# Neighbourhood bias masked on VectorE, the second layer's bias made in the first feed-forward, softmax maxima taken with the sign turned

## The chip, the cores and the metric

The kernel runs on one core of a Trainium2 chip. Its engines run side by side, each with its own queue in program order: PE (TensorE, matrix multiplications), DVE (VectorE), ACT (ScalarE), POOL (GpSimd) and SP (SyncE, here only the queue that issues transfers). The metric is the device time of one execution in microseconds; the median of the shown runs counts.

## The reference

Two identical layers act on 256 rows of width 1024. A layer is a mixer and a feed-forward with a gate, in float32:

```
h = rms_norm(x, n1);  proj = h @ w_in        # 1024 -> 2560, cut into qa ka va, qd kd vd, qc kc vc
out_a = neighbourhood_attention(rms(qa), rms(ka), va)        # 4 heads, a learned bias rpb per offset
out_d = dilated_window_attention(rot(rms(qd)), rot(rms(kd)), vd)   # 6 heads
out_c = gqa_block_attention(rot(rms(qc)), rot(rms(kc)), vc)        # 6 heads, 2 key heads
x = x + concat(rms(out_a), rms(out_d), rms(out_c)) @ w_out
h = rms_norm(x, n2);  g, u = split(h @ w_gate_up)            # 2 x 2816
x = x + (gelu(conv3(g)) * u) @ w_down
```

In all three attentions a score is q.k * 64^-0.5 plus a bias, and a softmax follows. The neighbourhood bias of a query and a key is rpb[head, row offset, column offset] inside a window of 16 columns, and minus infinity outside.

## The kernel before

**Arithmetic.** Every float32 weight or activation that goes to PE is split into a rounded part ("hi", cast by ACT) and the rest ("lo", subtracted by DVE), and a product takes two or three matmuls. Weights come in units of up to 1 MB through SP's queue into four `raw` buffers; a unit's split (`wp_hi`, `wp_lo`) is made while the unit two before it is multiplied.

**Stages of a layer.** First the norm's transposes (`act_hT`) and the projections dq, dk, dv, cq, ckv, aqk, av into PSUM banks `psa_a`. `normed` (line 840) makes each head's sum of squares (`small_ss`), on POOL the factor (`small_ms`, then `small_rstd` by a power), and on DVE the scaled `act_z`; `rotated` multiplies by cosine and sine tables that POOL makes from `const_rot` and the gains (`tables_d`, line 809: cdq, sdq, cdk, sdk; `tables_c`, line 824: ccq, scq, cck, sck). Then sixteen heads in the order 6 dilated ("d"), 6 grouped ("c"), 4 neighbourhood ("a"): scores in pairs into `psw_w`, softmax (`Head.softens`, line 942), transposes of the probabilities and their split (`act_ch`, `act_cl`), and the weighted sum with the values. Projections and output projections (`act_mixT`) fill PE between these. The feed-forward then runs eleven steps of gate, up and down.

**Softmax.** With a bias, one DVE operation (CUSTOM_DVE_ANT_0 in the profile, ISA in the lists of order below) adds it, scales, writes `act_s2k` and keeps the row's maximum, which a second small instruction writes to `small_mx`. Without one (group c) DVE reduces the maximum of the scores. For each head a DVE multiplication then makes `small_nm`, minus the maximum (times the scale in group c), which ACT's exponential takes as its bias. DVE's reciprocal and two ACT scalings finish the head.

**Neighbourhood bias of a layer.** `na_load` (line 692) brings 28 rows of 31 numbers (`act_few`); `na_repeat` (line 706) scales them on POOL by 8, copies them 64 times along the free axis into `act_nab` (28x1984) and writes that to a scratch in DRAM (`dram_scr`); `na_diagonals` (line 716) reads it back along diagonals with two transfers, so that each query partition has its bias for 28 (head, row offset) pairs and 64 columns. `na_bias_mask` (line 1076) adds the column mask `const_na` in three operations of 9x64 columns on POOL. There is one `act_nab` buffer; the second layer's is made from steps 2, 3 and 4 of the first feed-forward on in program order.

**What sets the order.** The kernel first records every operation with what it reads and writes (`Plan.add`, line 241). `Plan.order` (line 289) then lays the work out by list scheduling: of all operations that are ready it takes the one that can start first by its own cost function (`cost`, line 396) and handover times, ties by program position. `emit` (line 388) issues them in that order; line 393 is the line of nearly every instruction in the profile. So any changed cost or dependence can move work on every engine.

Of the kernel before, what the change touches and what calls it, by code (L numbers as in the profile page):

```python
# [11 lines left out]
F32 = mybir.dt.float32  # L12
F32R = mybir.dt.float32r
I32 = mybir.dt.int32
AF = mybir.ActivationFunctionType
# [200 lines left out]

class Plan:
    def __init__(self, tc):
        self.tc, self.ops, self.shift, self.burst, self.bursts = tc, [], 0, None, {}
        for name, short in (("tensor", "PE"), ("scalar", "ACT"), ("vector", "DVE"), ("gpsimd", "POOL"), ("sync", "SP")):  # L220
            setattr(self, name, PlanEngine(self, short, getattr(tc.nc, name)))

# [10 lines left out]
    @contextmanager  # L233
    def together(self):

        self.burst = len(self.bursts)
        self.bursts[self.burst] = []
        yield
        self.burst = None

    def add(self, engine, method, args, kw):
        o = Op()
# [37 lines left out]
            v.tile.reads.append((i, v.footprint()))  # L280
        for v in outs:
            v.tile.writes.append((i, v.footprint()))
        o.before.discard(i)
        o.left = len(o.before)
        for j in o.before:
# [150 lines left out]
def encoder_kernel(  # L436
# [268 lines left out]

    def na_repeat(l):
        rows_ = nabs[l].rearrange("p r c -> p (r c)")[:NR]
        nc.gpsimd.tensor_scalar(nabs["few"], nabs["few"], ISCALE, None, ALU.mult)
        nc.gpsimd.tensor_copy(
            rows_.rearrange("p (n c) -> p n c", c=RPB_C),  # L710
            nabs["few"].unsqueeze(1).to_broadcast([NR, GRID_W, RPB_C]),
        )
        nabs["scr"] = dram.tile([NR, GRID_W * RPB_C], F32, tag="scr", name=f"scr{l}")
        nc.sync.dma_start(nabs["scr"], rows_)

    def na_diagonals(l):
        scr = nabs["scr"]
        for i in range(2):
            nc.sync.dma_start(
                nabs[l][i * GRID_W : (i + 1) * GRID_W, i : i + NR],  # L720
                scr.strided(15, [[RPB_C - 1, GRID_W], [GRID_W * RPB_C, NR], [1, GRID_W]]),
            )

    load(0)
    for l in range(DEPTH):
# [68 lines left out]
        if l == 0:  # L794
# [9 lines left out]
            na_load(0)  # L804
            gq = gq.rearrange("p (l a d) -> p l a d", l=DEPTH, d=HD)
            gk = gk.rearrange("p (l a d) -> p l a d", l=DEPTH, d=HD)


        def tables_d(which, g):
            cd = act.tile([P, NT, HD], F32, tag=f"cd{which}", name=f"cd{which}{l}", bufs=1)  # L810
            sd = act.tile([P, NT, 16], F32, tag=f"sd{which}", name=f"sd{which}{l}", bufs=1)
            b = lambda v: v.unsqueeze(1).to_broadcast([P, NT, v.shape[1]])
            nc.gpsimd.tensor_tensor(cd, rot[:, :, 0:64], b(g[:, l, 1]), op=ALU.mult)
            for i in range(2):
                o, n = (8 * i, 8 * (1 - i)), 8
                nc.gpsimd.tensor_tensor(
                    sd[:, :, o[0] : o[0] + n],
                    rot[:, :, 64 + o[0] : 64 + o[0] + n],
                    b(g[:, l, 1, o[1] : o[1] + n]),
                    op=ALU.mult,  # L820
                )
            return cd, sd

        def tables_c(which, g):
            cc = act.tile([P, NT, HD], F32, tag=f"cc{which}", name=f"cc{which}{l}", bufs=1)
            sc = act.tile([P, NT, HD], F32, tag=f"sc{which}", name=f"sc{which}{l}", bufs=1)
            b = lambda v: v.unsqueeze(1).to_broadcast([P, NT, v.shape[1]])
            nc.gpsimd.tensor_tensor(cc, rot[:, :, 80:144], b(g[:, l, 2]), op=ALU.mult)
            for i in range(4):
                o, n = (16 * i, 16 * (i ^ 1)), 16  # L830
                nc.gpsimd.tensor_tensor(
                    sc[:, :, o[0] : o[0] + n],
                    rot[:, :, 144 + o[0] : 144 + o[0] + n],
                    b(g[:, l, 2, o[1] : o[1] + n]),
                    op=ALU.mult,
                )
            return cc, sc


        def normed(ps, nh, t, name):  # L840
# [96 lines left out]
        class Head:  # L937
# [4 lines left out]
            def softens(self, sps):  # L942

                name, bias = self.name, self.bias
                self.p = p = act.tile([P, NT, S], F32, tag="s2k", name=f"p_{name}", bufs=NS2K)
                nm = small.tile([P, NT], F32, tag="nm", name=f"nm_{name}")
                mx = small.tile([P, NT], F32, tag="mx", name=f"mx_{name}")
                rs = small.tile([P, NT], F32, tag="rs", name=f"rs_{name}")
                if bias is not None:
                    sb = act.tile([P, NT, S], F32, tag="s2k", name=f"sb_{name}", bufs=NS2K)  # L950
                    for t in range(NT):
                        nc.vector.tensor_tensor_reduce(
                            sb[:, t], sps[t], bias[t], SCALE, -3e38, ALU.add, ALU.max, mx[:, t : t + 1]
                        )
                    nc.vector.tensor_scalar_mul(nm, mx, -1.0)
                    for t in range(NT):
                        nc.scalar.activation(
                            p[:, t], sb[:, t], AF.Exp, bias=nm[:, t : t + 1], accum_out=rs[:, t : t + 1]
                        )
                else:  # L960
                    for t in range(NT):
                        nc.vector.reduce_max(mx[:, t : t + 1], sps[t], axis=AX.X)
                    nc.vector.tensor_scalar_mul(nm, mx, -SCALE)
                    for t in range(NT):
                        nc.scalar.activation(
                            p[:, t], sps[t], AF.Exp, bias=nm[:, t : t + 1], scale=SCALE,
                            accum_out=rs[:, t : t + 1],
                        )
                nc.vector.reciprocal(rs, rs)
                for t in range(NT):  # L970
                    nc.scalar.activation(p[:, t], p[:, t], AF.Copy, scale=rs[:, t : t + 1])
# [56 lines left out]
        LOW, HIGH = slice(0, HD), slice(HD, P)  # L1028

        def prep_d(which, g):  # L1030
            cd, sd = tables_d(which, g)
# [7 lines left out]
            turned["d" + which] = by_pairs(which, "d", H_DIL // 2, [hold["d" + which, t] for t in range(NT)])  # L1039

        def prep_c(which, g):
            cc, sc = tables_c(which, g)
# [33 lines left out]
        def na_bias_mask():  # L1076
            for i in range(1, NR, 9):
                nv = nabs[l][:, i : i + 9]
                nc.gpsimd.tensor_tensor(
                    nv, nv, na_mask.unsqueeze(1).to_broadcast([P, 9, GRID_W]), op=ALU.add  # L1080
                )

        def na_bias(h):
# [201 lines left out]
        NA_STEPS = {2: na_load, 3: na_repeat, 4: na_diagonals}  # L1285
        for kind, s in FFN:
            if kind == "G" and l + 1 < DEPTH and s in NA_STEPS:
                NA_STEPS[s](l + 1)
            if kind == "G":
                gate(s)  # L1290
            elif kind == "U":
# [85 lines left out]
```

## Time and profile before

| what | value |
|---|---|
| median of three runs (lowest to highest) | 625.4 us (625.36 to 627.85) |
| profiled execution, its own time | 626.01 us |
| its span, first to last instruction | 624.2 us |
| granted TensorE clock | 1.00 |
| PE, DVE, ACT, POOL busy | 608.7, 490.3, 430.6, 83.3 us |
| layer 0 attention and projections | up to about 148 us |
| layer 0 feed-forward | about 148 to 317 us |
| layer 1 attention and projections | about 317 to 438 us |

Times in rows are microseconds from the span's start; a mean is in ns. In a timeline row the first number is the start, the second the length, and the bracket is the engine's idle time before it with what ended it. In a group's row busy time and the mean of one stand after the bar, then the idle time before them. Matmuls overlap in PE's pipeline, so that PE counts as busy across gaps of a few tenths of a microsecond. A chain is followed back from the last instruction to what released each step.

### The profile page before, as it was taken

How to read it: one execution, taken by the hardware profiler on the slowest of the kernel's cores; microseconds unless marked ns; L12 is line 12 of the kernel's file. 1: busy time of each engine (PE TensorE's matmuls, PEld its weight loads, DVE VectorE, ACT ScalarE, POOL GpSimd, SP SyncE). 2: the span in 40 equal slices, each digit the busy share in tenths (PEclk: the TensorE clock that was granted, in tenths of full speed). 3: DMA queues.
4: the chain of work that ended last, by engine and by line, in shares of the span. 5: the costliest groups of instructions: out<-in, count | busy, mean ns of one | idle time of the engine just before them, and what ended most of it. 6: DMA issues, size and time to landing. Idle time of an engine off the chain costs nothing.

```text
span 624.2 us, 9846 instructions
## 1 busy us (share of the span) xinstructions
PE 608.7 (98%) x3496; PEld 525.0 (84%) x3496; DVE 490.3 (79%) x1026; ACT 430.6 (69%) x1064; POOL 83.3 (13%) x131
## 2 busy tenths in 40 slices
PE   8999999989999999999999999998999999999997
PEld 6998888778888888888899979786888888888885
DVE  4889889798777777777867798978877777877775
ACT  6887998677655655565588799888765655566552
POOL 2764231340000000000023210312000000000000
PEclk9999999999999999999999999999999999999999
DMA  8794312866555555555444632043565655555511
GB/s 279 262 287 154 102 40 96 249 154 213 189 177 178 199 202 202 179 172 173 153 145 154 225 102 85 34 138 136 202 207 199 202 188 170 187 199 188 170 49 67
DMA packets 81345, 104.66 MB, mean 168 GB/s; under 512 B 9464, under 2 KB 68952, under 8 KB 81296
## 3 DMA queue, kind: packets, MB, share of 16 engines
q1 hardware_dynamic: 80720, 103.51, 51.0%
q8 instruction: 27, 0.44, 0.3%
q10 hardware_dynamic: 576, 0.53, 0.3%
q14 instruction: 22, 0.18, 0.1%
HBM read 102.54 MB, written 1.49 MB: 167 GB/s over the span
## 4 chain that ended last, share of the span: by engine, by line
PE 86%; ACT 4%; DVE 4%; DMA 3%; POOL 1%; issue 1%; SPq 0%; ACTq 0%; POOLq 0%; DVEq 0%
PE psw_w L393 47%; PE psa_a L393 39%; ACT act_s2k L393 2%; DMA act_nab<-dram_scr 1%; DVE wp_lo L393 1%; DMA dram_scr<-act_nab 1%; DVE act_s2k L393 1%; POOL small_rstd L393 1%; DVE act_hT L393 1%; DMA act_s2k<-in_norm_g_dram 1%; POOL act_nab L393 0%; ACT L393 0%; ACT wp_hi L393 0%; DVE const_x L393 0%; DVE act_z L393 0%
## 5 line engine op out<-in xcount | busy, mean ns | idle before, releaser
L393 DVE TENSOR_TENSOR wp_lo<-wp_raw,wp_hi 128x512 fp32r<-128x512 f32 (+2 forms) x348 | 248.3, 742 | 50.9 <-ACT wp_hi L393 49.1
L393 PE MATMUL psw_w<-act_hT,wp_hi 128*128 128x512 f32 x704 | 247.4, 396 | 4.7 <-DVE act_hT L393 4.7
L393 ACT CAST wp_hi<-wp_raw 128x512 fp32r<-128x512 f32 (+2 forms) x348 | 213.7, 658 | 25.1 <-PE psw_w L393 15.6
L393 PE MATMUL psw_w<-act_hT,wp_lo 128*128 128x256 f32 x704 | 195.7, 279 | 0.0
L393 PEld LDWEIGHTS psw_w<-act_hT,wp_hi 128*128 128x128 f32 x704 | 131.8, 188 | 36.8 <-DVE act_hT L393 5.9
L393 PEld LDWEIGHTS psw_w<-act_hT,wp_lo 128*128 128x128 f32 x704 | 132.6, 188 | 1.1
L393 PE MATMUL psa_a<-wp_hi,act_hT 128*128 128x384 f32 (+2 forms) x448 | 114.9, 335 | 0.0
L393 ACT COPY act_s2k<-psw_w 128x256 f32<-128x256 f32 x88 | 32.3, 372 | 81.1 <-PE psw_w L393 81.1
L393 PEld LDWEIGHTS psa_a<-wp_hi,act_hT 128*128 128x128 f32 x448 | 78.6, 190 | 2.3
L393 PE MATMUL psa_a<-wp_lo,act_hT 128*128 128x384 f32 (+2 forms) x224 | 74.6, 334 | 0.0
L393 PE MATMUL psa_a<-wp_lo,act_ch 128*128 128x512 f32 x176 | 69.5, 395 | 0.0
L393 PE MATMUL psa_a<-wp_hi,act_ch 128*128 128x512 f32 x176 | 69.4, 394 | 0.0
L393 PE MATMUL psa_a<-wp_hi,act_cl 128*128 128x512 f32 x176 | 66.2, 395 | 0.2 <-DVE act_cl L393 0.2
L393 DVE TENSOR_TENSOR act_s2k<-psw_w,act_s2k 128x256 f32<-128x256 f32 x88 | 36.8, 422 | 30.6 <-ACT act_s2k L393 30.0
L393 PEld LDWEIGHTS psa_a<-wp_lo,act_hT 128*128 128x128 f32 x224 | 42.5, 190 | 2.1 <-DVE wp_lo L393 1.0
L393 PEld LDWEIGHTS psa_a<-wp_hi,act_cl 128*128 128x128 f32 x176 | 33.2, 188 | 8.3 <-DVE act_cl L393 0.6
L393 PEld LDWEIGHTS psa_a<-wp_hi,act_ch 128*128 128x128 f32 x176 | 33.1, 188 | 7.7
L393 PEld LDWEIGHTS psa_a<-wp_lo,act_ch 128*128 128x128 f32 x176 | 33.1, 188 | 6.9
L393 DVE SCALAR_TENSOR_TENSOR act_s2k<-act_s2k,act_cw,act_s2k 128x255 f32<-128x255 f32 x88 | 36.7, 476 | 1.4 <-ACT act_s2k L393 1.3
L393 ACT ACTIVATE act_s2k<-act_s2k,act_cw 128x256 f32<-128x256 f32 x44 | 24.1, 595 | 13.3 <-DVE act_s2k L393 13.3
L393 POOL TENSOR_TENSOR small_rstd<-small_ms,const_mh 128x6 f32<-128x6 f32 (+2 forms) x26 | 31.3, 1203 | 2.1
L393 ACT ACTIVATE act_s2k<-act_s2k,small_rs 128x256 f32<-128x256 f32 x64 | 28.8, 506 | 3.3 <-DVE small_rs L393 3.3
(110 smaller groups left out, 764.0 us busy)
## 6 DMA issues: line engine op xcount, KB each, us to landing
wp_raw<-in_w_gate_up_dram SPq DMA_DIRECT2D x44, 1024.0 KB, 5.0
wp_raw<-in_w_down_dram SPq DMA_DIRECT2D x22, 1024.0 KB, 4.8
wp_raw<-in_w_in_dram SPq DMA_DIRECT2D x14, 768.0 KB, 4.8
wp_raw<-in_w_in_dram SPq DMA_DIRECT2D x8, 1024.0 KB, 5.5
wp_raw<-in_w_out_dram SPq DMA_DIRECT2D x8, 768.0 KB
wp_raw<-in_w_out_dram SPq DMA_DIRECT2D x4, 512.0 KB, 3.7
act_nab<-dram_scr SPq DMA_DIRECT2D x4, 448.0 KB, 6.7
out_dram<-const_x SPq DMA_DIRECT2D x4, 256.0 KB, 2.0
```

What stands on the lines that cost most here:

```text
L393: getattr(o.engine.real, o.method)(*map(real, o.args), **{k: real(v) for k, v in o.kw.items()})
```

## The change

Four things are edited.

- *Mask.* `na_bias_mask` becomes a DVE operation that multiplies the bias by 8 and adds the mask in one pass (three of them per layer); POOL's scaling of `act_few` goes.
- *Softmax sign.* With a bias, the DVE operation scales by -1/8 and keeps the minimum, which is `small_nm` itself; the exponential takes the scale -1. Without one, the maximum is reduced negated, and the scale 1/8 is multiplied into the gain from which POOL makes ccq and scq (one small POOL operation per layer). The multiplication that made `small_nm` goes, 32 in all.
- *Second layer's bias.* `not_before("SP")` makes each of its three steps depend, for the planner's order, on the last SP operation recorded before it.
- *Second layer's tables.* All of them are recorded in step 4 of the first feed-forward, behind POOL's last operation recorded so far; the functions now stand outside the layer loop. Before, the planner was free to place them in the first layer's attention.

```diff
+    @contextmanager
+    def not_before(self, engine):
+        self.behind = max(i for i, o in enumerate(self.ops) if o.engine.name == engine)
+        yield
+        self.behind = None
...
+        if self.behind is not None:
+            o.before.add(self.behind)
         o.before.discard(i)
...
     def na_repeat(l):
         rows_ = nabs[l].rearrange("p r c -> p (r c)")[:NR]
-        nc.gpsimd.tensor_scalar(nabs["few"], nabs["few"], ISCALE, None, ALU.mult)
...
+    def tables_c(l, which):
+        g = gains_of[which][:, l, 2]
+        if which == "q":
+            nc.gpsimd.tensor_scalar(g, g, SCALE, None, ALU.mult)
...
+    def tables_of(l):
+        for which in "qk":
+            tables["d" + which, l] = tables_d(l, which)
+        for which in "qk":
+            tables["c" + which, l] = tables_c(l, which)
...
                     for t in range(NT):
                         nc.vector.tensor_tensor_reduce(
-                            sb[:, t], sps[t], bias[t], SCALE, -3e38, ALU.add, ALU.max, mx[:, t : t + 1]
+                            sb[:, t], sps[t], bias[t], -SCALE, 3e38, ALU.add, ALU.min, nm[:, t : t + 1]
                         )
-                    nc.vector.tensor_scalar_mul(nm, mx, -1.0)
                     for t in range(NT):
                         nc.scalar.activation(
-                            p[:, t], sb[:, t], AF.Exp, bias=nm[:, t : t + 1], accum_out=rs[:, t : t + 1]
+                            p[:, t], sb[:, t], AF.Exp, bias=nm[:, t : t + 1], scale=-1.0,
+                            accum_out=rs[:, t : t + 1],
                         )
                 else:
                     for t in range(NT):
-                        nc.vector.reduce_max(mx[:, t : t + 1], sps[t], axis=AX.X)
-                    nc.vector.tensor_scalar_mul(nm, mx, -SCALE)
+                        nc.vector.reduce_max(nm[:, t : t + 1], sps[t], axis=AX.X, negate=True)
                     for t in range(NT):
                         nc.scalar.activation(
-                            p[:, t], sps[t], AF.Exp, bias=nm[:, t : t + 1], scale=SCALE,
-                            accum_out=rs[:, t : t + 1],
+                            p[:, t], sps[t], AF.Exp, bias=nm[:, t : t + 1], accum_out=rs[:, t : t + 1]
                         )
...
         def na_bias_mask():
             for i in range(1, NR, 9):
                 nv = nabs[l][:, i : i + 9]
-                nc.gpsimd.tensor_tensor(
-                    nv, nv, na_mask.unsqueeze(1).to_broadcast([P, 9, GRID_W]), op=ALU.add
+                nc.vector.scalar_tensor_tensor(
+                    nv, nv, ISCALE, na_mask.unsqueeze(1).to_broadcast([P, 9, GRID_W]), ALU.mult, ALU.add
                 )
...
             if kind == "G" and l + 1 < DEPTH and s in NA_STEPS:
-                NA_STEPS[s](l + 1)
+                with nc.not_before("SP"):
+                    NA_STEPS[s](l + 1)
+            if kind == "G" and l + 1 < DEPTH and s == 4:
+                with nc.not_before("POOL"):
+                    tables_of(l + 1)
```

The recorded order moves on every engine. Three places matter for what follows. The first is layer 0, where the mask of the bias stood in POOL's queue ahead of the norm factors of the cq projection (`small_ms`, `small_rstd`). POOL before:

```order
L393 TENSOR_TENSOR act_cdk_353<-const_rot_171,const_gk_184 128x128
L393 TENSOR_TENSOR act_sdk_359<-const_rot_171,const_gk_184 128x2x8 x2
L393 TENSOR_TENSOR act_nab_370<-act_nab_370,const_na_214 128x576 x2
L393 TENSOR_SCALAR small_ms_296<-small_ss_279,small_he_253 128x6
L393 TENSOR_TENSOR small_rstd_313<-small_ms_296,const_mh_83 128x6
L393 TENSOR_SCALAR small_ms_330<-small_ss_311,small_he_253 128x6
L393 TENSOR_TENSOR small_rstd_336<-small_ms_330,const_mh_83 128x6
L393 TENSOR_TENSOR act_nab_370<-act_nab_370,const_na_214 128x576
```

DVE at the same place now:

```order
L402 TENSOR_TENSOR wp_lo_140<-wp_raw_93,wp_hi_130 128x512 x4
L402 SCALAR_TENSOR_TENSOR act_nab_367<-act_nab_367,const_na_214 128x576 x2
L402 TENSOR_TENSOR wp_lo_246<-wp_raw_138,wp_hi_235 128x512
L402 TENSOR_TENSOR act_z_334<-psa_a_302,small_rstd_313 128x384
L402 ISA act_s2k_190,small_nm_675<-psw_w_123,const_dil_207 128x256
L402 ISA small_nm_675 128x1
L402 TENSOR_TENSOR act_sw_346<-act_z_334,act_scq_510 128x6x16 x4
```

Two of the three mask operations now stand in DVE's queue, between two weight splits and ahead of the first softmax; on POOL the factors follow the first layer's tables directly.

The second place is SP's queue in the first feed-forward, with the transfers of the second layer's bias. Before:

```order
L393 DMA wp_raw_93<-in_w_gate_up_dram 128x8x256
L393 DMA dram_scr_458<-act_nab_370 28x1984
L393 DMA wp_raw_138<-in_w_down_dram 128x2x1024
L393 DMA act_nab_370<-dram_scr_458 64x28x64 x2
L393 DMA wp_raw_157<-in_w_gate_up_dram 128x8x256
```

And now:

```order
L402 DMA act_few_194<-in_rpb_dram 28x1x31
L402 DMA wp_raw_164<-in_w_down_dram 128x2x1024
L402 DMA wp_raw_93<-in_w_gate_up_dram 128x8x256
L402 DMA wp_raw_138<-in_w_gate_up_dram 128x8x256
L402 DMA wp_raw_157<-in_w_down_dram 128x2x1024
L402 DMA dram_scr_454<-act_nab_367 28x1984
L402 DMA wp_raw_164<-in_w_gate_up_dram 128x8x256
L402 DMA act_nab_367<-dram_scr_454 64x28x64 x2
```

Before, the scratch write stood ahead of the first w_down load of the layer; now it stands behind the fourth, and the gather behind one more gate_up load.

The third place is the end of each attention stage on PE (layer 0 shown; `const_ident` rows are transposes of probabilities, `const_v` rows weighted sums, `mixT` rows output projections). Before:

```order
L393 MATMUL psw_w_144<-const_ident_81,act_s2k_190 128x128
L393 MATMUL psa_a_162<-wp_lo_246,act_mixT_hi_910 128x512
L393 MATMUL psw_w_144<-const_ident_81,act_s2k_190 128x128 x3
L393 MATMUL psa_a_162<-wp_hi_235,act_mixT_lo_928 128x512
L393 MATMUL psa_a_162<-wp_hi_235,act_mixT_hi_910 128x512
L393 MATMUL psa_a_162<-wp_lo_246,act_mixT_hi_910 128x512
L393 MATMUL psa_a_162<-wp_hi_235,act_mixT_lo_928 128x512
L393 MATMUL psa_a_162<-wp_hi_235,act_mixT_hi_910 128x512
L393 MATMUL psa_a_162<-wp_lo_246,act_mixT_hi_910 128x512
L393 MATMUL psa_a_162<-wp_hi_235,act_mixT_lo_928 128x512
L393 MATMUL psw_w_119<-const_ident_81,act_s2k_121 128x128
```

And now:

```order
L402 MATMUL psw_w_119<-const_ones_85,act_sqm_1007 128x1 x2
L402 MATMUL psw_w_144<-const_ident_81,act_s2k_121 128x128
L402 MATMUL psw_w_123<-act_cl_765,const_v_87 128x256
L402 MATMUL psw_w_123<-act_ch_748,const_v_100 128x256
L402 MATMUL psw_w_123<-act_ch_748,const_v_87 128x256
L402 MATMUL psw_w_123<-act_cl_765,const_v_87 128x256
L402 MATMUL psw_w_123<-act_ch_748,const_v_100 128x256
L402 MATMUL psw_w_144<-const_ident_81,act_s2k_121 128x128 x3
L402 MATMUL psw_w_123<-act_ch_858,const_v_87 128x256
L402 MATMUL psw_w_119<-const_ident_81,act_s2k_150 128x128 x3
L402 MATMUL psw_w_123<-act_cl_870,const_v_87 128x256
```

Before, output projections stood between the last heads' transposes; now transposes and sums of two heads follow one another without any (17 rows in all), and the projections come behind them.

More of the change, by code (lines that the diff above doesn't have):

```diff
@@ L218, in __init__ @@
     def __init__(self, tc):
-        self.tc, self.ops, self.shift, self.burst, self.bursts = tc, [], 0, None, {}
+        self.tc, self.ops, self.shift, self.burst, self.bursts, self.behind = tc, [], 0, None, {}, None
         for name, short in (("tensor", "PE"), ("scalar", "ACT"), ("vector", "DVE"), ("gpsimd", "POOL"), ("sync", "SP")):
@@ L722, in na_diagonals, with tables_d @@
             )
+    def tables_d(l, which):
+        cd = act.tile([P, NT, HD], F32, tag=f"cd{which}", name=f"cd{which}{l}", bufs=1)
+        sd = act.tile([P, NT, 16], F32, tag=f"sd{which}", name=f"sd{which}{l}", bufs=1)
+        b = lambda v: v.unsqueeze(1).to_broadcast([P, NT, v.shape[1]])
+        nc.gpsimd.tensor_tensor(cd, gains_of["rot"][:, :, 0:64], b(gains_of[which][:, l, 1]), op=ALU.mult)
+        for i in range(2):
+            o, n = (8 * i, 8 * (1 - i)), 8
+            nc.gpsimd.tensor_tensor(
+                sd[:, :, o[0] : o[0] + n],
+                gains_of["rot"][:, :, 64 + o[0] : 64 + o[0] + n],
+                b(gains_of[which][:, l, 1, o[1] : o[1] + n]),
+                op=ALU.mult,
+            )
+        return cd, sd
+    def tables_c(l, which):
+        g = gains_of[which][:, l, 2]
+        if which == "q":
+            nc.gpsimd.tensor_scalar(g, g, SCALE, None, ALU.mult)
+        cc = act.tile([P, NT, HD], F32, tag=f"cc{which}", name=f"cc{which}{l}", bufs=1)
+        sc = act.tile([P, NT, HD], F32, tag=f"sc{which}", name=f"sc{which}{l}", bufs=1)
+        b = lambda v: v.unsqueeze(1).to_broadcast([P, NT, v.shape[1]])
+        nc.gpsimd.tensor_tensor(cc, gains_of["rot"][:, :, 80:144], b(g), op=ALU.mult)
+        for i in range(4):
+            o, n = (16 * i, 16 * (i ^ 1)), 16
+            nc.gpsimd.tensor_tensor(
+                sc[:, :, o[0] : o[0] + n],
+                gains_of["rot"][:, :, 144 + o[0] : 144 + o[0] + n],
+                b(g[:, o[1] : o[1] + n]),
+                op=ALU.mult,
+            )
+        return cc, sc
+    gains_of, tables = {}, {}
+    def tables_of(l):
[3 more added lines that the diff above has]
+            tables["c" + which, l] = tables_c(l, which)
     load(0)
@@ L806, in encoder_kernel @@
             gk = gk.rearrange("p (l a d) -> p l a d", l=DEPTH, d=HD)
[L809 to L815, printed above, removed]
-                nc.gpsimd.tensor_tensor(
[L817 to L837, printed above, removed]
+            gains_of.update(q=gq, k=gk, rot=rot)
         def normed(ps, nh, t, name):
@@ L946, in softens @@
                 nm = small.tile([P, NT], F32, tag="nm", name=f"nm_{name}")
-                mx = small.tile([P, NT], F32, tag="mx", name=f"mx_{name}")
                 rs = small.tile([P, NT], F32, tag="rs", name=f"rs_{name}")
@@ L1030, in prep_d @@
         def prep_d(which, g):
-            cd, sd = tables_d(which, g)
+            if ("d" + which, l) not in tables:
+                tables["d" + which, l] = tables_d(l, which)
+            cd, sd = tables["d" + which, l]
             for t in range(NT):
@@ L1041, in prep_c @@
         def prep_c(which, g):
-            cc, sc = tables_c(which, g)
+            if ("c" + which, l) not in tables:
+                tables["c" + which, l] = tables_c(l, which)
+            cc, sc = tables["c" + which, l]
             nh = H_GQ if which == "q" else H_GKV
@@ L1078, in na_bias_mask @@
                 nv = nabs[l][:, i : i + 9]
-                nc.gpsimd.tensor_tensor(
-                    nv, nv, na_mask.unsqueeze(1).to_broadcast([P, 9, GRID_W]), op=ALU.add
+                nc.vector.scalar_tensor_tensor(
+                    nv, nv, ISCALE, na_mask.unsqueeze(1).to_broadcast([P, 9, GRID_W]), ALU.mult, ALU.add
                 )
```

## The prediction

> **What bounds the kernel now.** I read the totals first, then the chain that ended last, then the waits and the timelines of the two attention stages.
>
> ```profile
> PE 608.7 (98%) x3496; PEld 525.0 (84%) x3496; DVE 490.3 (79%) x1026; ACT 430.6 (69%) x1064; POOL 83.3 (13%) x131
> PE 86%; ACT 4%; DVE 4%; DMA 3%; POOL 1%; issue 1%; SPq 0%; ACTq 0%; POOLq 0%; DVEq 0%
> 148.00:317.00 169.00, 168.80 (x886) 143.41 (x885) 128.06 (x216) 101.09 (x187) 0.00 (x0) 1.00 0.56 186
> 360.00:400.00 40.00, 39.17 (x275) 33.45 (x275) 35.82 (x109) 37.27 (x105) 7.29 (x10) 1.00 0.25 81
> ```
>
> The last two rows are stretches of the span: length, then PE, PEld, DVE, ACT and POOL busy, PE clock, DMA share, GB/s. In a feed-forward (148 to 317) PE works 168.80 of 169 us at full clock, so nothing that VectorE sheds there can shorten it. In attention (360 to 400) DVE is busy 35.82 of 40 us and ACT 37.27: both are nearly full beside PE. PE's 39.17 there hides gaps, since pipelined matmuls overlap; the chain, taken within a stretch, shows them better. Here it is for layer 0 (60 to 148) and layer 1 (336 to 440):
>
> ```profile
> by line: PE psa_a L393 39.3%; PE psw_w L393 30.6%; DVE wp_lo L393 8.9%; DVE act_s2k L393 5.2%; issue 5.1%; DVE act_hT L393 3.1%; ACT act_s2k L393 2.1%; DVE act_cl L393 1.6%; ACT L393 1.5%; POOL act_sqm L393 0.8%; ACT act_sqm L393 0.7%; ACT
> by line: PE psa_a L393 47.4%; PE psw_w L393 31.7%; ACT act_s2k L393 8.3%; ACT act_ch L393 1.6%; issue 1.5%; ACT wp_hi L393 1.5%; ACT L393 1.2%; ACT act_hT L393 1.2%; ACT const_v L393 1.2%; POOL small_rstd L393 1.0%; DVE act_hT L393 0.9%; DV
> ```
>
> The chain leaves PE for 30.1% of 88 us, 26 us, and for 20.9% of 104 us, 22 us. Only from these can the change win. The clearest place is earlier, in layer 0, where the chain (start, length, what) runs through the neighbourhood bias; the last row is of PE's timeline, with the idle time before it in brackets:
>
> ```profile
> 30.10 5.37 DMA dram_scr<-act_nab
> 36.24 8.25 DMA act_nab<-dram_scr
> 44.65 2.81 POOL act_nab L393 x2
> 47.56 0.61 POOL small_ms L393
> 48.24 1.35 POOL small_rstd L393
> 51.53 1.64 DVE act_z L393
> 53.28 0.52 ACT act_s2k L393
> 53.84 0.33 PE L393 MATMUL psw_w<-const_ident,act_s2k 128*128 128x128 f32 x1 [1.12 <-ACT act_s2k L393]
> ```
>
> GpSimd waits for the gather, masks two thirds, and only then makes the cq norm's factor that stands behind the mask in its queue; PE stops for 1.12 us at the end of it.
>
> **The change part by part.** Durations come from the profiled execution, 626.01 us (span 624.2 and 1.8 around it), 0.6 above the median of the three runs, 625.4.
>
> *(a) The mask leaves GpSimd.* While a GpSimd pass over the bias runs, VectorE operations stretch:
>
> ```profile
> 46.07 1.95 DVE L393 TENSOR_TENSOR wp_lo<-wp_raw,wp_hi 128x512 fp32r<-128x512 f32 x1 [1.27 <-ACT wp_hi L393]
> 51.33 1.42 POOL L393 TENSOR_TENSOR act_nab<-act_nab,const_na 128x576 f32<-128x576 f32 x1
> 51.45 1.72 DVE L393 TENSOR_TENSOR act_z<-act_z,act_ccq 128x384 f32<-128x384 f32 x1
> 128.58 3.73 DVE L393 TENSOR_TENSOR wp_lo<-wp_raw,wp_hi 128x512 fp32r<-128x512 f32 x4
> 128.94 1.61 POOL L393 TENSOR_TENSOR act_nab<-act_nab,const_na 128x576 f32<-128x576 f32 x1 [6.58 <-DMA act_nab<-dram_scr]
> 132.75 0.50 PE L393 MATMUL psw_w<-act_hT,wp_hi 128*128 128x512 f32 x1 [1.94 <-DVE act_hT L393]
> L393 DVE TENSOR_TENSOR wp_lo<-wp_raw,wp_hi 128x512 fp32r<-128x512 f32 x240 | 161.6, 702 | 18.2 <-ACT wp_hi L393 16.4
> ```
>
> A wp_lo split of mean 702 ns takes 1.95 us, and the act_z product 1.72 us. At 51 us this meets the waiting factor: I count PE's 1.12 us as gone, **-1.1** (between 0, if a new wait takes its place, and 2.2, the time by which the factor can come sooner: 47.56 against 45.38, when ACT has done the first tile's squares and turns to the cast shown below). At 128.58 four splits take 3.73 us where four means come to 2.8; the new order puts one split more ahead of the act_hT operation on which PE waits 1.94 us. **-0.9** (0 to 1.9).
>
> *(b) The mask joins VectorE.* Six operations of 576 columns with a scalar are new there. The nearest rows are the split above (702 ns, 512 columns) and the convolution step below (476 ns, 255 columns): 257 columns cost 226 ns, so 576 cost 0.76 us.
>
> ```profile
> L393 DVE SCALAR_TENSOR_TENSOR act_s2k<-act_s2k,act_cw,act_s2k 128x255 f32<-128x255 f32 x88 | 36.7, 476 | 1.4 <-ACT act_s2k L393 1.3
> 45.38 0.65 ACT L393 CAST wp_hi<-wp_raw 128x512 fp32r<-128x512 f32 x1
> 35.48 1.73 SPq L393 DMA_DIRECT2D act_nab<-dram_scr  x2
> ```
>
> In layer 0 the first two stand just ahead of the split of 46.07. VectorE idles 1.27 us before it, since ACT's cast only starts at 45.38; the gather issued at 35.48 ended at 44.49 by the chain. So 1.27 of their 1.5 us fall into idle time and the data is there. The third stands among the softmaxes of heads 2 and 3, uncovered. Together 1.0 us of VectorE time; at the chain's share for engines other than PE, 30%, **+0.3** (0 to 1.0, and far more if the gather is late: a rival). Behind these operations wait all splits and softmaxes of the stage.
>
> The Trainium skill, SBUF — State Buffer, section SBUF: two separate sides, speaks against the move: the port pair of VectorE and GpSimd is an exclusive lock for a whole instruction, and a VectorE operation with two SBUF inputs takes it too. By that rule the first two masks would hold the cq factor on GpSimd for up to 1.5 us; the gain of the factor shrinks from 2.2 to 0.7 us, and the first term from 1.1 to 0.7. The stretched rows above agree with the lock.
>
> *(c) The sign.* Thirty-two multiplications for nm go; their reductions and exponentials stay as many.
>
> ```profile
> L393 DVE TENSOR_SCALAR small_nm<-small_mx 128x2 f32<-128x2 f32 x32 | 6.5, 203 | 0.0
> L393 DVE TENSOR_REDUCE small_mx<-psw_w 128x1 f32<-128x256 f32 x24 | 8.9, 416 | 3.0 <-PE psw_w L393 3.0
> L393 DVE CUSTOM_DVE_ANT_0 act_s2k<-psw_w,const_dil 128x256 f32<-128x256 f32 x24 | 9.4, 415 | 0.0
> 110.74 1.26 DVE L393 TENSOR_SCALAR small_nm<-small_mx 128x2 f32<-128x2 f32 x1
> ```
>
> 6.5 us of VectorE, always between a maximum and its exponential. If it counted only at the chain's share for other engines (0.3 and 0.21 of 3.25 us a layer) it would give 1.7; if whole, 6.5. Most softmaxes lie beside output-projection or projection matmuls, so I stay near the low end: **-2.5**. That the minimum and the negated reduction cost what their counterparts cost has no row; if these 24 and 24, and the 16 more that read act_nab, doubled from 0.42 us, VectorE would carry 27 us more.
>
> *(d) The second layer's bias and tables* move from layer 0's attention into its feed-forward: GpSimd's copy of 1.83 us at 110, the products for the tables, and the three bias transfers on SP's queue.
>
> ```profile
> 110.14 1.83 POOL L393 COPY act_nab<-act_few 28x1984 f32<-28x1984 f32 x1 [1.37 <-DVE small_ss L393]
> 111.40 0.91 ACT L393 ACTIVATE act_s2k<-act_s2k,small_rs 128x256 f32<-128x256 f32 x2
> 172.68 0.37 SPq L393 DMA_DIRECT2D wp_raw<-in_w_down_dram  x1
> 189.95 0.42 DVE L393 TENSOR_TENSOR act_s2k<-psw_w,act_s2k 128x256 f32<-128x256 f32 x1 [0.62 <-ACT act_s2k L393]
> 191.93 1.22 DVE L393 TENSOR_TENSOR wp_lo<-wp_raw,wp_hi 128x1024 fp32r<-128x1024 f32 x1 [1.55 <-ACT wp_hi L393]
> ```
>
> The copy held nm for 1.26 us, but ACT scaled until 112.2 anyhow: **-0.3** (0 to 1.05). In the feed-forward the scratch write now follows the w_down load of 172.68 and the gather the gate_up load after it, some 5.5 us on; with 8.25 us as in layer 0 it lands near 187. The mask stands behind the addition of 189.95, in the 1.55 us that VectorE idles before the split of 191.93. VectorE is idle 41 of 169 us there, so copy, tables and masks cost 0 (up to 1.5 if they meet one step of 16.8 us).
>
> Sum: -1.1 -0.9 +0.3 -2.5 -0.3 = -4.5; 626.0 - 4.5 = 621.5 for a profile, and 0.6 less for the median: **620.9 us**, 0.7% faster.
>
> **The rivals.** *The wait moves (0.28).* The planner has rewritten the order of both attention stages; if ACT's 37.27 of 40 us sets the pace there, VectorE's relief gives nothing, and the mask merely changes engines. For it: the layer 1 chain, where ACT act_s2k has 8.3% and VectorE hardly a row; against it: the PE stops of 1.12 and 1.94 us that GpSimd's passes cause. Only the first two terms less the third stay: 1.7, or 623.7. The Trainium skill, Perfetto Trace Analysis, section Optimizing Scalar/DVE Operations, warns in this sense that work moved between GpSimd and VectorE may not help.
>
> *It counts whole (0.16).* All 6.5 us of nm sit on the path, and the later waits shrink with them: 4 us more, 616.9. For it: each nm stands alone between DVE and ACT; against: ACT's own load.
>
> *Slower: a bare tail (0.12).* In the new PE order, transposes, weighted sums and a group sum of the last neighbourhood heads stand 17 rows together in each layer, with no output-projection matmul between them, where one to seven stood between such groups before. A head then shows its cast, transposes and subtraction:
>
> ```profile
> L393 ACT CAST act_ch<-psw_w 128x512 fp32r<-128x512 f32 x32 | 18.8, 588 | 10.0 <-PE psw_w L393 7.3 <-DVE wp_lo L393 1.7 <-ACT wp_hi L393 0.6
> 113.21 0.49 PE L393 MATMUL psw_w<-const_ident,act_s2k 128*128 128x128 f32 x3
> L393 DVE TENSOR_TENSOR act_cl<-psw_w,act_ch 128x512 fp32r<-128x512 f32 x32 | 21.8, 683 | 2.9 <-ACT act_ch L393 2.6
> ```
>
> 0.59 + 0.68 + 0.5, with its two scalings (0.91 by the row at 111.40), are 2.7 us a head: two heads, two layers, 10.7 us lost, 631.6. It decides from 7.6 us, 1.9 a head (628.5). Against it: more projection matmuls now follow the last sum, where before PE stood waiting. A gather that lands late belongs to the same side: at 44.8 us, each us of delay beyond VectorE's idle time stops the stage.
>
> **How the numbers follow.** The forecast holds 0.44, from 618.5 to 622.3. What can be told from no change is 0.5%, 3.1 us. Faster: forecast and the whole nm, 0.60. Same: the wait moves, 0.28. Slower 0.12. The range reaches from the deeper case to most of the second: 615.5 to 626.0; outside lie a little of the deep case, of the second, and the bare tail.
>
> **What would show it.** Right: GpSimd's cq factor near 47 instead of 48.2 to 49.6; no VectorE operation of the attention stretched past 1.2 us except at the first copy (25 us); PE without the stops of 1.12 and 1.94 us; the stretch from 336 to 440 shorter by a us or two; the feed-forward at 169. Wrong: a VectorE wait on the gather at 45 or 190; DVE's minimum or negated reduction well above 0.42 us; PE stops in the last pairs.

## The result, and the profile after

The changed kernel takes **618.49 us** (median of four runs, 617.32 to 619.27) against 625.73 for the kernel before in the same session: ratio 0.9876, interval 0.9848 to 0.9904, so 1.2% faster. The forecast was 620.9. The profiled execution takes 618.73 us with a span of 616.9, where before had 626.01 and 624.2: 7.3 us to be found.

From the page of the kernel after: busy times and counts, and the chain that ended last, by engine.

```profile
PE 607.5 (98%) x3496; PEld 525.4 (85%) x3496; DVE 487.1 (79%) x1000; ACT 429.8 (70%) x1064; POOL 78.1 (13%) x125
PE 93%; ACT 3%; DVE 2%; DMA 1%; issue 1%; ACTq 0%
```

PE does the same 3,496 matmuls. What has changed is how often the end hangs on another engine: PE's share of the chain goes from 86% to 93%. VectorE sheds 26 instructions (32 multiplications go, 6 masks come) but only 3.2 us of busy time. By stage, the chain of the kernel after in layer 0 (60 to 148) and in layer 1 (336 to 440), and the row of the feed-forward:

```profile
by line: PE psw_w L402 43.1%; PE psa_a L402 37.0%; ACT act_s2k L402 8.5%; DVE wp_lo L402 2.3%; issue 2.0%; DVE act_hT L402 1.9%; ACT act_ch L402 1.2%; DVE small_nm L402 1.0%; DVE act_z L402 0.8%; DVE const_x L402 0.7%; ACT wp_hi L402 0.6%; 
by line: PE psa_a L402 49.9%; PE psw_w L402 36.3%; ACT act_s2k L402 6.2%; DVE wp_lo L402 1.9%; DVE act_hT L402 1.7%; issue 1.5%; ACT act_ch L402 1.0%; DVE const_x L402 0.6%; ACT wp_hi L402 0.5%; ACT act_mixT_hi L402 0.3%; ACT act_sqm L402 0
148.00:317.00 169.00, 169.00 (x892) 144.16 (x891) 130.34 (x220) 102.22 (x192) 11.97 (x21) 1.00 0.59 186
```

The chain leaves PE for 19.9% of layer 0's stretch (30.1% before) and 13.8% of layer 1's (20.9%). In layer 0 it is VectorE's `wp_lo` that shrinks, 8.9% to 2.3%; in layer 1 the rows of ScalarE. The feed-forward is as full as it was.

Where the 7.3 us lie shows when the starts of the same matmul are compared in PE's timelines of the two kernels:

| start of | before | after | difference |
|---|---|---|---|
| first scores, layer 0 | 46.17 | 45.99 | -0.2 |
| second scores | 58.65 | 56.91 | -1.7 |
| first gate matmul, layer 0 | 126.89 | 124.12 | -2.8 |
| its hundredth | 153.57 | 149.75 | -3.8 |
| last of the feed-forward | 303.96 | 300.14 | -3.8 |
| first gate matmul, layer 1 | 433.62 | 425.68 | -7.9 |
| last of the second feed-forward | 609.04 | 601.71 | -7.3 |

So layer 0 gives 3.8 us, 0.2 of them ahead of the first scores, its feed-forward nothing from the hundredth gate matmul on, layer 1 another 3.5 to 4.1.

The start of layer 0's gain, in the timelines of GpSimd and VectorE after:

```profile
45.45 0.55 POOL L402 TENSOR_SCALAR small_ms<-small_ss,small_he 128x6 f32<-128x6 f32 x1 [9.56 <-ACT act_s2k L402]
46.09 1.71 POOL L402 TENSOR_TENSOR small_rstd<-small_ms,const_mh 128x6 f32<-128x6 f32 x1
44.44 1.43 DVE L402 SCALAR_TENSOR_TENSOR act_nab<-act_nab,const_na 128x576 f32<-128x576 f32 x2
47.84 0.56 DVE L402 TENSOR_TENSOR act_z<-psa_a,small_rstd 128x384 f32<-128x384 f32 x1 [1.25 <-POOL small_rstd L402]
```

The cq factor now waits for ScalarE's squares alone. It is done at 47.80 instead of 49.59, and the masks lie in VectorE's idle time ahead of it. The end of layer 0's gain is the start of its feed-forward; the chain (start, length, what) of before, in part, then of after:

```profile
133.87 2.27 DVE wp_lo L393 x2
136.60 0.41 DVE act_s2k L393
139.48 1.20 DVE wp_lo L393 x2
147.53 0.69 DVE act_cl L393
153.16 11.29 PE psw_w L393 x64
```

```profile
128.90 0.45 DVE act_hT L402
129.39 14.38 PE psw_w L402 x82
143.77 5.56 PE psa_a L402 x24
149.34 11.29 PE psw_w L402 x64
```

Before, VectorE ran behind for 20 us after the stage's end. GpSimd's three masks for layer 1 lay beside its splits at 129 to 136 us, and six of these took 6.61 us where six means of 0.70 come to 4.2. Now PE is the chain from 129.39 on.

### The profile page after: what moved, and what is told of

It is laid out like the page before. It is cut to its first block, busy times and chain, and to the rows that moved or that the text cites. A ratio compares the mean times of both kernels' runs of the same rounds, so it can differ in the third digit from the quotient of the medians.

```text
span 616.9 us, 9838 instructions
## 1 busy us (share of the span) xinstructions
PE 607.5 (98%) x3496; PEld 525.4 (85%) x3496; DVE 487.1 (79%) x1000; ACT 429.8 (70%) x1064; POOL 78.1 (13%) x125
## 4 chain that ended last, share of the span: by engine, by line
PE 93%; ACT 3%; DVE 2%; DMA 1%; issue 1%; ACTq 0%
PE psw_w L402 49%; PE psa_a L402 44%; ACT act_s2k L402 2%; DMA const_x<-in_x_dram 1%; DVE wp_lo L402 1%; DVE act_hT L402 1%; ACT act_ch L402 0%; DVE const_x L402 0%; ACTq L402 0%; ACT wp_hi L402 0%; DVE small_nm L402 0%; ACT act_mixT_hi L402 0%; DVE act_z L402 0%; ACT act_sqm L402 0%; DVE small_rs L402 0%
## 5 line engine op out<-in xcount | busy, mean ns | idle before, releaser
L402 DVE TENSOR_TENSOR wp_lo<-wp_raw,wp_hi 128x512 fp32r<-128x512 f32 (+2 forms) x348 | 244.5, 732 | 48.2 <-ACT wp_hi L402 46.3
L402 PE MATMUL psa_a<-wp_hi,act_hT 128*128 128x384 f32 (+2 forms) x448 | 113.4, 333 | 0.0
L402 ACT ACTIVATE act_s2k<-act_s2k 128x512 f32<-128x512 f32 x22 | 13.9, 632 | 22.4 <-DVE act_s2k L402 22.4
```

Source lines behind the costliest of these rows:

```text
L402: getattr(o.engine.real, o.method)(*map(real, o.args), **{k: real(v) for k, v in o.kw.items()})
```

## The experiments

Theory A: the removed multiplication itself saves time, wherever it stood. Theory B: what stood in its place sets the pace in the old order, and any gain comes through the order that the planner now writes. The mask and the placement have rivals of their own: that they only move work from engine to engine.

| kernel | median us | ratio to before (interval) | first scores | layer 0 | layer 1 |
|---|---|---|---|---|---|
| after | 618.49 | 0.9876 (0.9848, 0.9904) | -0.2 | -3.8 | -4.1 |
| e1_sign_old_order | 627.50 | 1.0001 (0.9983, 1.0019) | +1.0 | +0.5 | 0.0 |
| e2_nm_back | 622.08 | 0.9927 (0.9906, 0.9948) | -0.4 | -2.0 | -3.1 |
| e3_sign_alone | 624.17 | 0.9956 (0.9938, 0.9973) | -1.6 | -0.2 | -4.3 |
| e4_no_sign | 625.20 | 0.9979 (0.9960, 0.9999) | +0.2 | -1.1 | +0.4 |
| e5_mask_alone | 626.18 | 1.0000 (0.9978, 1.0023) | +0.1 | -1.5 | -0.1 |
| e6_mask_pool | 620.37 | 0.9884 (0.9858, 0.9911) | -1.2 | -3.2 | -3.8 |
| e7_no_place | 620.38 | 0.9889 (0.9857, 0.9922) | +1.5 | -1.6 | -4.1 |
| e8_pool_passes | 620.39 | 0.9890 (0.9858, 0.9922) | -0.4 | -2.4 | -4.1 |
| n1_before_handover | 627.61 | 1.0005 (0.9990, 1.0019) | +0.1 | +2.8 | -0.3 |
| n2_before_actcost | 627.11 | 1.0008 (0.9992, 1.0024) | +0.1 | +2.2 | -1.1 |
| n1_after_handover | 620.33 | 0.9879 (0.9857, 0.9900) | +0.1 | -1.8 | -4.2 |
| n2_after_actcost | 619.38 | 0.9864 (0.9846, 0.9883) | +0.5 | -3.1 | -3.8 |

The last three columns come from each kernel's one trace, against the trace of before: the start of the first scores, that of the hundredth gate matmul of the first feed-forward ("layer 0", which includes the first), and what is added from there to the first gate matmul of the second. They show places, and the ratios decide. The differences at the first scores, from -1.6 to +1.5 us, are there from about 12 us on; e1, which keeps the whole order of before on PE, starts 1.0 later. So they are taken as differences between executions, and what layer 0 itself gives is read by subtracting them. The two shifted orders of before had a lower clock at 120 to 130 us (last section). The kernel before had medians of 625.7 to 627.0 in the four sessions, so kernels of different sessions are compared by ratio.

### The sign in the old order

The instructions of before, engine by engine in their old order, with the 32 multiplications left out; the group's scale goes into the rotation constants.

```diff
-                nc.vector.tensor_scalar_mul(nm, mx, -1.0)        # planned, not issued
-   tensor_tensor_reduce(..., SCALE, -3e38, ALU.add, ALU.max, mx)
+   tensor_tensor_reduce(..., -SCALE, 3e38, ALU.add, ALU.min, mx)
-   activation(..., AF.Exp, bias=nm)
+   activation(..., AF.Exp, bias=mx, scale=-1.0)
```

> The kernel before in its own recorded order on all engines; only the 32 multiplications that make small_nm are not issued, the minimum or negated maximum is the exponential's bias, and the scale of group c sits in the rotation constants (its root in those of q and of k). Theory A (the instruction counts: 6.5 us of VectorE between a maximum and its exponential is on the path in part): 2.5 us faster than before, 1.5 to 6.5. Theory B (the new order counts: the shorter chain only pays where the planner lays everything out anew): within 1 us of before.

Measured: 1.0001. Thirty-two VectorE instructions fewer, 6.5 us of busy time, give nothing that the interval (about 1 us either way) can tell. Why shows in layer 1, in the chain of before and then of this kernel:

```profile
384.47 0.47 ACT const_v L393
384.94 4.38 ACT act_s2k L393 x14
```

```profile
384.88 0.47 ACT const_v L395
385.36 4.38 ACT act_s2k L395 x14
```

Fourteen ScalarE instructions (exponentials, their sums, scalings, squares) run back to back for 4.38 us in both. The maxima were there before ScalarE came to them, with the multiplication or without. VectorE's early result waited in ScalarE's queue. Theory B holds here.

### The multiplication put back in the new order

After's order, with 38 small VectorE copies of `small_nm` put in, 26 of two columns and 12 of one, which the exponentials read.

```diff
+   nc.vector.tensor_scalar_mul(nm2[:, c : c + 2], nm, 1.0)
-   activation(..., bias=nm[:, t : t + 1], ...)
+   activation(..., bias=nm2[:, c + t : c + t + 1], ...)
```

> The changed kernel in its own order on all engines, with a VectorE copy of small_nm put back between each maximum and its exponentials (38 small operations, 0.2 us each by the rows of before). Theory A: 2.5 us slower than the changed kernel, 1.5 to 6.5, so near 621. Theory B: within 1 us of the changed kernel's 618.5.

Measured: 0.9927, 0.5% slower than after's 0.9876 (622.08 and 618.49 us by medians of two sessions; the intervals do not meet). The groups of the copies, and the chain of layer 1, where two of them now stand on it:

```profile
L412 DVE TENSOR_SCALAR const_nm<-small_nm 128x2 f32<-128x2 f32 x26 | 4.7, 179 | 0.9
L410 DVE TENSOR_SCALAR const_nm<-small_nm 128x1 f32<-128x1 f32 x12 | 1.8, 154 | 0.4
```

```profile
383.81 0.76 DVE small_nm L404 x2
384.59 0.18 DVE const_nm L412
384.79 1.03 ACT act_s2k L404 x4
```

ScalarE's waits for the bias of its exponentials (in total, times, longest) tell the same for the whole kernel. Here they are of before, of after, and of this kernel:

```profile
ACT act_s2k L393 <- DVE small_nm L393: 0.3, 1, 0.3
ACT act_s2k L402 <- DVE small_nm L402: 1.9, 6, 0.6
ACT act_s2k L404 <- DVE const_nm L412: 4.3, 9, 1.2
ACT act_s2k L404 <- DVE const_nm L410: 0.7, 2, 0.5
```

In the old order ScalarE waited 0.3 us in all for the multiplication, in the new one 1.9 without it and 5.0 with the copies: 3.1 us more.

The same kind and amount of work, 6.5 us, that was free to remove from the old order costs about 3 us in the new one. Both theories were half right: the instruction counts where VectorE is waited for, and only the new order makes it so. In layer 1, 3.1 of the 4.1 us remain with the copies in: that part is the order's own.

### One part at a time, planned anew

```diff
 e3_sign_alone: before + the softmax of after (and the scale in POOL's gain); mask and placement as before
 e4_no_sign:    after with the softmax of before; mask and placement as after
 e5_mask_alone: before + na_bias_mask of after, POOL's scaling of act_few gone
```

> Only the sign of the maximum is changed (mask on GpSimd, second layer's bias and tables where they were free to go before), laid out anew by the planner. Theory A: as the same edit in the old order, 2.5 us faster than before. Theory B: clearly more than that edit in the old order, 4 us or more, with the gain in layer 1 as large as the whole change's 3.5 us. The stops at 52 and 131 us that GpSimd's mask causes stay by both.

> The whole change without the sign: mask on VectorE, second layer's bias and tables in the first feed-forward, small_nm made by its own multiplication. By the terms of the prediction 2.0 us faster than before (1.1 + 0.9 + 0.3 - 0.3), all of it in layer 0, and layer 1 as before. By theory B a reordering alone may move it by 2 us either way, in layer 1 too.

> Only the mask moves from GpSimd to VectorE (with the scaling of few left out); sign, and the second layer's bias and tables, as before; laid out anew. By the prediction's terms 1.1 + 0.9 - 0.3 = 1.7 us faster than before, all of it in layer 0. If only the new order counts, anywhere within 2 us of before, layer 1 moving too.

Measured: sign alone 0.9956, mask and placement 0.9979, mask alone 1.0000. The parts add to 0.65%, the whole is 1.24%. The sign alone gains 2.8 us, which is theory A's 2.5 and not the 4 or more of theory B; but by the traces it is layer 1 that gains, the whole 4 us, as theory B has it. Layer 0 loses: from the first scores to the hundredth gate matmul it takes 1.4 us longer than before. Where shows against e6 (next part), which has the same order on PE up to 111 us but neither the copy nor the masks of layer 1 there. At the seventh pair of scores the two are 0.4 us apart (96.06 and 96.48), as at the first; at the first gate matmul the sign alone is 2.1 us behind (127.17 against 125.04), at the hundredth 3.0 (153.39 against 150.37). The timelines of GpSimd and VectorE of the sign alone at that place:

```profile
105.54 2.24 POOL L393 COPY act_nab<-act_few 28x1984 f32<-28x1984 f32 x1 [7.44 <-DVE small_nm L393]
106.07 2.25 DVE L393 TENSOR_TENSOR wp_lo<-wp_raw,wp_hi 128x512 fp32r<-128x512 f32 x1
132.98 5.12 POOL L393 TENSOR_TENSOR act_nab<-act_nab,const_na 128x576 f32<-128x576 f32 x3
133.38 1.59 DVE L393 TENSOR_TENSOR wp_lo<-wp_raw,wp_hi 128x512 fp32r<-128x512 f32 x1
137.07 1.59 DVE L393 TENSOR_TENSOR wp_lo<-wp_raw,wp_hi 128x512 fp32r<-128x512 f32 x1
```

Splits of 0.69 us take 2.25 beside the copy and 1.59 beside the masks, and the first of them stands on the chain. In before's order the copy of 110.14 had hit a multiplication that nobody waited for. So the copy's price is set by what happens to lie beside it. GpSimd can be held as well: in the same trace its addition of 128x2 at 128.31, 0.34 us in the mean of before, takes 3.64 us while six VectorE splits run back to back (128.20 to 131.90).

The mask alone is ahead by 1.2 us at the second scores (57.48) and by 1.5 at the hundredth gate matmul; its ratio does not tell that from nothing, where 1.7 us were expected. Its trace loses 1.6 us again at the start of the second feed-forward, where the clock was low (last section).

### One part taken away

```diff
 e6_mask_pool: after, with the mask of before on POOL (sign and placement stay)
 e7_no_place:  after, without not_before and tables_of (sign and mask stay)
```

> The changed kernel with the mask (and the scaling of few) back on GpSimd; sign turned, second layer's bias and tables in the feed-forward. By the terms the cq factor of layer 0 is late again and PE's stop near 52 us returns: 1.1 + 0.9 - 0.3 = 1.7 us slower than the changed kernel (620.2); layer 1 as in the changed kernel. If only the order counts: layer 1 moves by a us or more too.

> The changed kernel without the two placements: the planner may put the second layer's bias and tables into layer 0's attention again. By the terms 0.3 us slower than the changed kernel, and GpSimd's copy near 110 us stretches a VectorE operation there. A loss of 2 us or more would say that the placement carries the gain.

Measured: 0.9884 and 0.9889. Each alone keeps all but about 0.1% of the gain, less than the intervals tell apart, and by medians at most 2 us. Beside the sign's 0.9956 each brings some 0.7%, and the second of them hardly anything more. One thing is common to both: they take long passes of GpSimd away from VectorE's splits at the tail of layer 0. The placement moves copy and masks of layer 1 into the feed-forward; the mask's move takes the masks away, and leaves the copy wherever the planner puts it. That the move of the mask to VectorE is itself needed is not shown by the ratios. The traces, one each, point to what was expected for e6: PE's stop near 53 us comes back with 0.63 us, and from the first scores to the hundredth gate matmul e6 takes 1.6 us longer than after. For e7 it is 0.6, and the stretched operation that was expected there did not come: the planner puts the copy at 108.89 beside a VectorE that idles for 1.04 us, and no VectorE operation there takes over 0.69.

### GpSimd passes beside VectorE

After, with three GpSimd passes of 576 columns behind the second cq factor, over a buffer that nothing else uses.

```diff
+   for _ in range(3):
+       pool.tensor_tensor(idle, idle, ident[:, 0:64] (repeated 9 times), op=ALU.add)
```

> The changed kernel in its own order on all engines, with three GpSimd passes over a scratch tile of the bias's size (128x576, two inputs in SBUF, 1.4 to 1.9 us each in the profile of before) added behind the second cq factor of layer 0, where nothing waits for them. If GpSimd's passes stretch VectorE (the prediction's reading of the 1.95 and 1.72 us rows): up to three VectorE operations near 50 to 55 us take over 1.2 us, and the end comes 1 to 3 us later. If the waiting factor alone was the harm: VectorE's rows as in the changed kernel and no loss over 0.5 us.

Measured: 0.9890, 620.39 us; the trace is 1.4 us behind after's from the second scores to the first feed-forward. GpSimd and VectorE of this kernel:

```profile
49.31 4.83 POOL L527 TENSOR_TENSOR const_idle<-const_idle,const_ident 128x576 f32<-128x576 f32 x3
49.43 1.73 DVE L402 TENSOR_TENSOR act_z<-act_z,act_ccq 128x384 f32<-128x384 f32 x1
51.08 0.41 DVE L402 CUSTOM_DVE_ANT_0 act_s2k<-psw_w,const_dil 128x256 f32<-128x256 f32 x1
51.43 1.45 DVE L402 TENSOR_TENSOR act_z<-act_z,act_sw 128x384 f32<-128x384 f32 x1
53.67 1.02 DVE L402 TENSOR_TENSOR wp_lo<-wp_raw,wp_hi 128x512 fp32r<-128x512 f32 x1
```

The three operations whose inputs both lie in SBUF take 4.20 us instead of 1.79 (0.55, 0.55, 0.69); the one that reads PSUM keeps its 0.41. Of the 2.4 us that VectorE loses, PE loses 1.4 (1.6 counted from the first scores). The ratio alone would not tell this from after; the trace's place does. By the Trainium skill, SBUF — State Buffer, section SBUF: two separate sides, a VectorE operation with two SBUF inputs and a GpSimd operation that reads SBUF exclude each other for a whole instruction; these rows agree.

### Is it one lucky order?

Two constants of the planner, each in both kernels.

```diff
 n1: handover from DVE to ACT
-    160
+    180
 n2: ACT's extra cost for a scale or bias read from SBUF
-    extra = 93 *
+    extra = 103 *
```

> The kernel before, with one number of the planner changed that has no meaning on the chip: the handover from VectorE to ACT is taken as 180 ns instead of 160. The recorded order changes, the work doesn't. If orders of the same work differ by chance, this shows by how much: theory B expects up to 2 us either way; if the order is of no weight, within 0.5 us of before.

> The changed kernel with the handover from VectorE to ACT taken as 180 ns instead of 160 by the planner. If the change's gain is its own, this stays within 2 us of 618.5, and well below both variants of before; if the gain is one lucky order, it falls back towards 622 to 625.

> The kernel before, with another number of the planner changed: ACT's extra cost for a scale or bias read from SBUF is taken as 103 ns instead of 93. As the handover variant: within 0.5 us if the order is of no weight, up to 2 us either way if it is.

> The changed kernel with ACT's extra cost taken as 103 ns instead of 93 by the planner. As the handover variant of the changed kernel: near 618.5 if the gain is the change's own, 622 to 625 if it is one lucky order.

Measured: 1.0005 and 1.0008 for before, 0.9879 and 0.9864 for after. All three orders with the change are 1.2 to 1.4% faster than all three without. In layer 1 every replanned kernel with the sign gains 3.8 to 4.3 us, and none without it gains more than 1.1. An order that fits this well is not shown to be reachable without the sign, nor shown not to be.

## Why the prediction was right, and where not

**The forecast** had the sign of the change and the size within 2.4 us: 4.5 us were forecast, 7.2 measured. At 618.49 the time lies at the very edge of its case (618.5 to 622.3), and nearer to "it counts whole" (616.9) than to the forecast.

**(a) The mask leaves GpSimd: right.** The first -1.1 measured -1.6 between the first and the second scores, and -1.3 with the mask alone. The wait of 1.12 us is gone and no new one took its place. The second, -0.9, measured -1.06 between the first and the hundredth gate matmul of the feed-forward. PE's waits on `act_hT` after, in total, times and longest:

```profile
PE psw_w L402 <- DVE act_hT L402: 2.7, 2, 1.3
```

Before it was 4.7 in four, up to 1.9. The doubt that the prediction set beside this, that masks on VectorE would hold the factor on GpSimd, came out small here: the two factor instructions took 0.55 and 1.71 us, against 0.28 and 1.32 for the second tile's pair, beside which VectorE mostly reads PSUM, so 0.7 us together. Not counted was that the step by itself would not show in the time: mask alone 1.0000.

**(b) The mask joins VectorE: right.** Groups after: the masks, the minimum, the negated reduction.

```profile
L402 DVE SCALAR_TENSOR_TENSOR act_nab<-act_nab,const_na 128x576 f32<-128x576 f32 x6 | 4.4, 752 | 0.0
L402 DVE CUSTOM_DVE_ANT_0 act_s2k<-psw_w,const_dil 128x256 f32<-128x256 f32 x24 | 9.6, 418 | 0.3 <-PE psw_w L402 0.2
L402 DVE TENSOR_REDUCE small_nm<-psw_w 128x1 f32<-128x256 f32 x24 | 8.8, 417 | 1.0 <-PE psw_w L402 0.9
```

752 ns against 0.76 us worked out from two other shapes, and minimum and negated reduction cost what maximum and reduction did (415 and 416). The gather was never waited for.

**(c) The sign: the mis-sized term.** It was given as -2.5 for both layers, by taking the chain's share of the removed time. Layer 0 as a whole came out as summed (3.5 with three fifths of this term, 3.6 measured from the first scores), but not as a sum, and so in part by luck: the sign alone makes it 1.4 us slower, and beside mask and placement (e4 to after) it brings 2.3. Layer 1 should have given 1.0 and gave 3.5 to 4.1. The step that failed is the multiplication of 6.5 us by a share of the chain. The profile of before already held a better price: ScalarE waited 0.3 us in all for `small_nm`. In the old order the instruction was worth 0 (e1), in the new one about 3 us (e2), and the order itself another 3 in layer 1. The whole sign, from e4 to after, is worth 1.0%, some 6.4 us, as much as all of its busy time; "it counts whole" came near the number, but not because the instruction sat on the path whole. In e4, where the planner knows of the multiplication, ScalarE idles 0.2 us in all before its exponentials, and the time is still 6.4 us longer. The old chain in layer 1 left PE for ScalarE at 356.3, 384.5 and 420.2; the new one does it once before the stage's last norm, and PE's waits for `act_s2k`, 2.7 us in four before, are gone from its list:

```profile
402.17 0.59 ACT act_ch L402
402.75 3.58 ACT act_s2k L402 x12
410.44 0.48 ACT act_ch L402
```

The rival "the wait moves" named the right mechanism, ScalarE's queue, for the order of before. It missed that a planner which no longer reckons with a step of VectorE's between maximum and exponential lays ScalarE's work out differently.

**(d) The second layer's bias and tables: price right in the feed-forward, too low in the attention.** Timelines after, VectorE and SP's queue:

```profile
175.02 4.08 SPq L402 DMA_DIRECT2D act_nab<-dram_scr  x2
186.12 0.42 DVE L402 TENSOR_TENSOR act_s2k<-psw_w,act_s2k 128x256 f32<-128x256 f32 x1 [0.61 <-ACT act_s2k L402]
186.47 0.75 DVE L402 SCALAR_TENSOR_TENSOR act_nab<-act_nab,const_na 128x576 f32<-128x576 f32 x1
188.10 1.23 DVE L402 TENSOR_TENSOR wp_lo<-wp_raw,wp_hi 128x1024 fp32r<-128x1024 f32 x1 [0.88 <-ACT wp_hi L402]
```

The mask stands behind the named addition, without a wait, and takes its time from VectorE's idle 1.55 us; from the hundredth gate matmul on, both feed-forwards take what they took, to 0.3 us. But -0.3 was read from what the copy hit in the order of before. With the sign and the mask on GpSimd, leaving copy and masks in layer 0 costs 0.7% (e3 against e6); with the mask on VectorE, e7, hardly anything.

**A bare tail: the wait came, the loss did not.** The ScalarE stretch of 402 to 411 above is the pair of last heads that the rival spoke of; its twin in layer 0 lies at 100.6 to 109.4. The group sum behind it starts only 5.9 us sooner than before (411.18) where the scores ahead of it start 8.1 sooner (405.90): 2.2 us are paid there. They come back at once, since the projections now stand behind: the last weighted sum is again 8.05 us sooner (417.32). Work that PE had put between the heads, it has left for the end, where before it waited.

**What would show it.** VectorE has one stretched operation in the attention, 1.84 us at the first copy. The factor is done at 47.80, the feed-forward stretch is full. PE's stop of 1.12 us is gone; that of 1.94 has shrunk to 1.33, at 129.39. Layer 1 was to be a us or two shorter and is four.

## What to carry to other kernels

The share of the chain is no price per microsecond of removed work: the same 6.5 us were worth nothing in one order and half of themselves in another, so ask for each instruction who stands ready to use its result, and read how long that engine waits for it. Where a planner lays out the work, a small step on a dependence that recurs in every head is priced by replanning with it and without, and with the planner's constants shifted, not by its duration. Gains do not add: a stage runs ahead until its next obstacle, here GpSimd's passes beside VectorE's splits, and only with that gone too does the gain reach the end.

## What was not expected of the hardware

In four traces (e1, mask alone, and the two shifted orders of before) the granted clock fell to 0.83 over 10 us at the end of an attention stage; not in that of before, whose stop is the same. The stretch from 430 to 440 of e1 and of before (PE, PEld, DVE, ACT, POOL busy, then the clock), and PE's row at that place, of before and of after:

```profile
430.00:440.00 10.00, 7.77 (x37) 5.98 (x35) 7.99 (x14) 7.57 (x21) 1.98 (x4) 0.83 0.54 185
```

```profile
430.00:440.00 10.00, 7.18 (x43) 5.58 (x42) 9.64 (x19) 7.86 (x21) 1.85 (x3) 1.00 0.55 193
433.62 0.50 PE L393 MATMUL psw_w<-act_hT,wp_hi 128*128 128x512 f32 x1 [1.59 <-DVE act_hT L393]
```

```profile
425.68 0.50 PE L402 MATMUL psw_w<-act_hT,wp_hi 128*128 128x512 f32 x1
```

The first 33 gate matmuls of the layer take 9.87 us in e1 and 8.31 in before: 1.6 us. PE had stopped for 1.60 us just ahead in e1, as in before. After has no stop there (one of 1.34 us follows at 430.96), and its trace no fall.

The clock's records in the traces say more. Each of the five falls (one of the shifted orders has two) is half the clock for 3.413 us, in e1 from 434.81 to 438.22, and the stretches of full clock ahead of them (112.64, 310.61 and 423.25 us) are 33, 91 and 124 times that. So the clock changed on a grid of 3.413 us, whose place differs between executions. In e1 the whole stop (432.50 to 434.10) lies in the 3.413 us ahead of the fall, in which PE is busy for 1.59; in before the stop (432.03 to 433.62) lies astride a point of its grid, 432.87. The same stop thus stands ahead of a loss of 1.6 us in one execution and of none in another. This is not the whole rule: in e4, 1.35 of the stop's 1.59 us lie in one such stretch, and no fall follows. By the Trainium skill, TensorE: Matmul & The Clock Gate, section Part 1: The HAM clock gate, the clock is halved after an idle window of about 3.4 us; half the clock for 3.4 of 10 us is a mean of 0.83, which agrees, while the stop was shorter than the page's window. That the stop causes the fall is not shown.

It does not make the gain: of the kernel before's executions with a mean clock of 0.999 or more, the medians are 625.7 to 625.9 us in three sessions, and of after's three such 618.2, 7.5 to 7.7 us apart. It may hide a gain of the mask alone, where nine of ten executions had a lower mean clock than that, against five of twelve of before.
